# A ConvFFN whose down projection takes seven products of quarter matrices instead of eight, for 16 of 22 feature blocks

## The chip, the cores and the metric

The kernel runs on one core of one Trainium2 chip, as one launch. The metric is the device time of that launch in microseconds (us). Each engine of the core works through its own queue of instructions in order: TensorE (PE) does the matrix products and loads their weights (PEld), VectorE (DVE), ScalarE (ACT) and GpSimd (POOL) do elementwise work, and SyncE (SP) and POOL issue DMAs.

## The reference, cut to what matters

Two layers with different mixers; each is followed by the same ConvFFN. A prompt of 512 tokens and 8 samples of 8 tokens go through the same weights, 576 tokens in all.

```python
D_MODEL = 1024
D_FF = ((8 * D_MODEL // 3 + 255) // 256) * 256      # 2816 = 22 blocks of 128

def conv_ffn(h, hist, w_gate, w_up, conv_w, conv_b, w_down):
    gate = h @ w_gate
    padded = jnp.concatenate([hist, gate], axis=1)
    gc = causal_dwconv(padded, conv_w, conv_b)
    y = (jax.nn.silu(gc) * (h @ w_up)) @ w_down
    return y, padded[:, -(FFN_CONV_WIDTH - 1):]
```

## The kernel before, in words

Everything is kept with features on the 128 partitions and the 576 tokens along the free axis, in two halves of 288 (`HB`). The running sum lives in eight tiles `self.x[m]` of 128x576. Products are fp32 made of three matmuls on values split in two: a high part (`hi`, a copy that ScalarE rounds) and a low part (`lo`, the rest, subtracted on VectorE): hi·hi, hi·lo and lo·hi, added up in one PSUM bank. Every operand therefore costs one ScalarE and one VectorE instruction before TensorE can use it.

`ffn` handles one layer's ConvFFN. The first blocks of gate and up are done plainly (`lead`). The others go in pairs of feature blocks as **jobs** (class `Strassen`): 19 a layer, a Gate job and an Up job by turns. A job multiplies the two weight blocks with the 1024x576 input in seven products of quarters instead of eight. Its weight sums S1 to S4 are made by DMA: SP loads one quarter from HBM into a slot of SBUF, and POOL issues a second DMA that adds another on top. `alpha`, `beta` and `gamma` split the upper weights, (S1, S2) and (S3, S4) into hi and lo; p1 to p7 are the products, each of 12 matmuls. A Gate job ends in `gate_done` (convolution, SiLU, the new state), an Up job in `up_done`.

The **down projection** of the 22 blocks goes in six parts (`PARTS`): blocks 0 and 1, then four parts of four blocks (2 to 17), and the last four in `out_proj`. `down(p)` is a generator: each step does one output block m and one half of the tokens, and adds the bank to `self.x[m]` on VectorE (`add_x`). The loop over the jobs calls one step after p1, p3, p7 and p5 (`some(1)`), four a job, so a part of 16 steps lies beside four jobs; what is left of the part of blocks 14 to 17 behind the last job is done in one go (`some(16)`).

Weights come through three buffers `wr` (`weights_load`). Smaller things take slots from a list (`S`), 48 and 14 extra, given out in the order in which they were freed; a slot's new writer waits for its last reader. The tile framework orders the instructions of each engine itself, from the order of the code and its own idea of when inputs are there; the first matmul of a product is pinned to the order of the code.

Of the kernel before, what the change touches and what calls it, by code (L numbers as in the profile page):

```python
# [14 lines left out]
P = 128  # L15
# [9 lines left out]
PARTS = ((0, 2), (2, 6), (6, 10), (10, 14), (14, 18), (18, 22))  # L25

# [25 lines left out]
class Strassen:  # L52

    def __init__(self, b, job, n):
        self.b, self.nc, self.job = b, b.nc, job
        s = b.sr
        self.r, self.e, self.a = s[0][:, HALF[0]], s[1][:, HALF[0]], s[1][:, HALF[1]]

    def load(self):
        b = self.b
        up, low = self.job.src
        self.up = b.weights_load(up, 1024)
        s1, s2, s3, s4 = self.s = [b.S(f"st{i}", 512) for i in range(4)]
        for s, first, more in ((s1, low[:, 512:1024], low[:, 0:512]), (s2, up[:, 0:512], s1), (s4, up[:, 512:1024], s2),
                               (s3, up[:, 0:512], low[:, 0:512])):
            self.nc.sync.dma_start(s, first)
            self.nc.gpsimd.dma_start(s, more, accum_op=ADD)  # L69
        self.low = b.weights_load(low[:, 512:1024], 512)  # L70
        self.alpha()

    def sums(self, between=None):
        b = self.b
        if between:
            between()
        self.d = b.S("dh", 512, F32R), b.S("dl", 512, F32R)
        self.split(self.low[:, 0:512], *self.d)
# [22 lines left out]
    def gamma(self):  # L101
        self.w3 = self.two(self.s[3], self.s[2])
        self.b.free(self.s[3], self.s[2])
# [54 lines left out]
class Builder:  # L158
    NSLOT = 48
    EXTRA = 14  # L160

    def __init__(self, nc, tc, d, stack):
# [7 lines left out]
        self.rings = {"mm": [0, 1, 2, 3], "aux": [4, 5, 6, 7]}  # L170
        self.idle = list(range(self.NSLOT))
# [4 lines left out]
    def S(self, name, n=T, dt=F32, rows=P):  # L176

        i = self.idle.pop(0)
# [90 lines left out]
    def weights_load(self, src, n):  # L269
        raw = self.wp.tile([P, 1024], F32, tag="wr", bufs=3, name="wr")  # L270
# [275 lines left out]
    def ffn(self, l, next_norm):  # L546
        nc, d = self.nc, self.d
        self.rings = {"mm": [0, 1, 2, 3, 4, 5], "aux": [6, 7]}
        hist, so = self.S("fhist", NF * 16), self.S("fso", NF * 16)
# [30 lines left out]

        def up_done(f):
            y_of[f] = self.pair("y")
# [143 lines left out]

        todo = [Gate(LEAD_G), Up(LEAD_U)]
# [3 lines left out]
        self.sr = [self.S("st"), self.S("st")]  # L731
        tiles = iter(())
# [7 lines left out]
        for n, job in enumerate(todo + [None]):  # L740
# [35 lines left out]
            if ready < len(PARTS) - 1 and PARTS[ready][1] - 1 in y_of and n < len(todo):  # L776
                some(16)
                tiles = down(ready)
                ready += 1
            prev = new  # L780
        some(16)
        nc.sync.dma_start(d["ffn_s"][l], so)
        nc.sync.dma_start(d["ffn_p"][l], po)
        self.free(so, hist, self.sr, list(self.hq.values()))
# [1139 lines left out]
```

## Time and profile before

| | us |
|---|---|
| median of 3 runs (lowest to highest) | 1482.55 (1481.72 to 1483.52) |
| the profiled execution's own time | 1483.3 |
| its span in the trace | 1481.5 |
| busy in the span: DVE, ACT, POOL | 1119.0, 822.0, 304.1 |
| parts of four blocks beside four jobs, layer 0 | 323.85 to 393.91, to 463.95, to 534.20 |
| the last such part and its rest, layer 0 | 534.20 to 585.20 |
| the same four in layer 1, each from | 1191.47, 1261.54, 1331.41, 1401.49 |

In a row of groups stand the line of the kernel, the engine, the operation, the tile written and those read, the shapes and the count; then busy us and the mean ns of one; then the idle time of the engine before them and what ended it. A row of windows gives the stretch, its length, and the busy us (and instructions) of PE, PEld, DVE, ACT and POOL, then the granted TensorE clock, the DMA share and GB/s. A row of the timeline gives start, duration, engine, line, operation, tiles and count.

### The profile page before, as it was taken

Reading aid. Unit: us, or ns where it says so; the run is one execution under the profiler, and the core shown is the slowest. Engines: PE = TensorE matmul, PEld = TensorE weight load, DVE = VectorE, ACT = ScalarE, POOL = GpSimd, SP = SyncE. Lnnn points to the kernel's source line nnn. Section 1 sums busy time; section 2 is a strip of 40 time slices with the busy share of each in tenths; the row PEclk is TensorE's granted clock in tenths of the full one; section 3 lists DMA queues with packets and bytes.
Section 4 is the critical chain, followed back from the end, with each engine's and each line's share of the span. In section 5 each row is a group of like instructions: output and inputs, shape, how many; then the busy total and the mean of one; then the engine's idle time right before and its main releaser. Section 6 shows DMA issues by size and latency. Waiting matters only on the chain.

```text
span 1481.5 us, 29273 instructions
## 1 busy us (share of the span) xinstructions
PE 1459.2 (99%) x11179; PEld 1389.9 (94%) x11179; DVE 1119.0 (76%) x2121; ACT 822.0 (55%) x1659; POOL 304.1 (21%) x517
## 2 busy tenths in 40 slices
PE   8999999999999999999999999999999999999999
PEld 7967799999999999998988998997999999999998
DVE  7968799876666665878897777776989766666673
ACT  6357467655445543487764665665457554444450
POOL 0026211222222220011203102102022222232300
PEclk9999999999999999999999999999999999999999
DMA  7604553787777772136245245245366787877841
GB/s 228 164 29 118 160 133 100 195 212 197 184 200 197 191 191 69 58 121 199 72 154 178 86 124 165 86 146 166 105 172 176 193 217 184 211 195 179 212 113 65
DMA packets 120779, 227.60 MB, mean 154 GB/s; under 512 B 25518, under 2 KB 32558, under 8 KB 120638
## 3 DMA queue, kind: packets, MB, share of 16 engines
q1 hardware_dynamic: 98750, 185.87, 39.7%
q0 software_dynamic: 21888, 39.86, 16.3%
q8 instruction: 88, 1.44, 0.4%
q14 instruction: 53, 0.43, 0.1%
HBM read 190.54 MB, written 15.21 MB: 139 GB/s over the span
## 4 chain that ended last, share of the span: by engine, by line
PE 86%; DVE 6%; ACT 4%; DMA 2%; issue 1%; SPq 0%; ACTq 0%; POOL 0%; DVEq 0%
PE mm L313 15%; PE mm L317 15%; PE mm L316 15%; PE x L113 5%; PE x L116 5%; PE x L117 5%; PE y L116 3%; PE y L117 3%; PE y L113 3%; PE mm L622 2%; PE mm L618 2%; PE mm L621 2%; PE z L116 1%; PE z L113 1%; PE z L117 1%; DMA acb<-acd 1%
## 5 line engine op out<-in xcount | busy, mean ns | idle before, releaser
L313 PE MATMUL mm<-hh,wh 128*128 128x288 f32 x864 | 261.0, 303 | 6.0 <-ACT wh L284 5.4
L316 PE MATMUL mm<-hl,wh 128*128 128x288 f32 x864 | 258.8, 300 | 0.9 <-DVE hl L801 0.8
L317 PE MATMUL mm<-hh,wl 128*128 128x288 f32 x864 | 257.5, 298 | 0.5 <-DVE wl L285 0.5
L497 DVE TENSOR_TENSOR x<-x,mm 128x288 f32<-128x288 f32 x288 | 128.6, 449 | 77.6 <-PE mm L317 76.3
L313 PEld LDWEIGHTS mm<-hh,wh 128*128 128x128 f32 x864 | 163.6, 190 | 14.3 <-ACT wh L284 5.9
L313 PE MATMUL mm<-yh,vh 128*128 128x288 f32 x576 | 170.0, 295 | 0.0
L316 PE MATMUL mm<-yl,vh 128*128 128x288 f32 x576 | 169.9, 295 | 0.0
L317 PE MATMUL mm<-yh,vl 128*128 128x288 f32 x576 | 169.8, 295 | 0.0
L316 PEld LDWEIGHTS mm<-hl,wh 128*128 128x128 f32 x864 | 163.5, 189 | 4.4 <-issue 1.6
L317 PEld LDWEIGHTS mm<-hh,wl 128*128 128x128 f32 x864 | 163.6, 189 | 3.5 <-issue 1.6
L284 ACT ACTIVATE wh<-wr 128x1024 fp32r<-128x1024 f32 (+1 forms) x97 | 101.6, 1048 | 102.6 <-PE mm L316 79.0
L285 DVE TENSOR_TENSOR wl<-wr,wh 128x1024 fp32r<-128x1024 f32 (+1 forms) x97 | 119.5, 1236 | 36.3 <-ACT wh L284 35.5
L82 ACT ACTIVATE wh<-st 128x512 fp32r<-128x512 f32 x152 | 91.3, 626 | 57.8 <-PE z L116 36.0
L69 POOL DMA_DIRECT2D st<-st x76 | 67.5, 889 | 262.8 <-DMA st<-st 65.5
L313 PE MATMUL mm<-yh,wh 128*128 128x288 f32 x384 | 115.9, 302 | 0.7 <-DVE x L497 0.7
L317 PE MATMUL mm<-yh,wl 128*128 128x288 f32 x384 | 115.0, 300 | 0.0
L316 PE MATMUL mm<-yl,wh 128*128 128x288 f32 x384 | 114.9, 300 | 0.0
L83 DVE TENSOR_TENSOR wl<-st,wh 128x512 fp32r<-128x512 f32 x152 | 101.3, 688 | 15.9 <-ACT wh L82 12.3
L316 PEld LDWEIGHTS mm<-yl,vh 128*128 128x128 f32 x576 | 108.4, 188 | 0.0
L317 PEld LDWEIGHTS mm<-yh,vl 128*128 128x128 f32 x576 | 108.3, 188 | 0.0
L313 PEld LDWEIGHTS mm<-yh,vh 128*128 128x128 f32 x576 | 108.3, 188 | 0.0
L573 DVE SCALAR_TENSOR_TENSOR gconv<-gbuf,par,gconv 128x592 f32<-128x592 f32 x88 | 73.0, 832 | 32.2 <-ACT gconv L571 31.6
(409 smaller groups left out, 4306.4 us busy)
## 6 DMA issues: line engine op xcount, KB each, us to landing
st<-in_w_up SPq DMA_DIRECT2D x80, 256.0 KB, 4.3
wr<-in_w_down SPq DMA_DIRECT2D x80, 256.0 KB, 3.5
wr<-in_w_in_o SPq DMA_DIRECT2D x40, 512.0 KB, 3.6
st<-st POOLq DMA_DIRECT2D x76, 256.0 KB, 4.7
st<-in_w_gate SPq DMA_DIRECT2D x72, 256.0 KB, 4.6
wr<-in_w_gate SPq DMA_DIRECT2D x26, 512.0 KB, 4.3
wr<-in_w_up SPq DMA_DIRECT2D x24, 512.0 KB, 4.1
st<-in_w_up POOLq DMA_DIRECT2D x40, 256.0 KB, 4.7
```

The source lines that it names most:

```text
L82: nc.scalar.activation(hi, src, AF.Copy)
L83: nc.vector.tensor_tensor(lo, src, hi.bitcast(F32), op=SUB)
L113: m = nc.tensor.matmul(out, hi[:, ws], xh, start=first and k == 0, stop=False, skip_group_check=skip)
L116: nc.tensor.matmul(out, hi[:, ws], xl, start=False, stop=False, skip_group_check=skip)
L117: nc.tensor.matmul(out, lo[:, ws], xh, start=False, stop=k == 3, skip_group_check=skip)
L284: nc.scalar.activation(hi[:, a:b], raw[:, a:b], AF.Copy)
L285: nc.vector.tensor_tensor(lo[:, a:b], raw[:, a:b], hi[:, a:b].bitcast(F32), op=SUB)
L313: first = nc.tensor.matmul(out, hi[:, ws], xh[:, sl], start=i == 0, stop=False)
L316: nc.tensor.matmul(out, hi[:, ws], xl[:, sl], start=False, stop=False)
L317: nc.tensor.matmul(out, lo[:, ws], xh[:, sl], start=False, stop=i == n - 1)
L497: nc.vector.tensor_tensor(self.x[m][:, sl], self.x[m][:, sl], p[:, :HB], op=ADD)
L573: nc.vector.scalar_tensor_tensor(cv[:, :592], g[:, k:592 + k], w(k), cv[:, :592], op0=MUL, op1=ADD)
```

## The change

For the four parts of four blocks (`SEVEN`), `down7` replaces `down`. It takes two output blocks m and m+1 and four feature blocks at a time as a 2x2 matrix of quarters, and the activations as 2x2 too (two blocks by two, left and right half of the tokens), and makes the result in seven products of 6 matmuls where there were eight. For this it adds weight sums S1 to S4 on VectorE, sums of activations (T1 to T4, once a part), splits of each, and more additions to `self.x`: a product that belongs to two quarters of the result is continued in its bank after it has been added once. A pair of output blocks takes four yields: two products, two, two, one. `up_done` splits only the left half of a part's first two blocks; the rest is split in `down7` (`operand`).

To make room, the jobs keep S3 and S4 in the buffer of the upper weights (`ring_up`, two of the three `wr`): POOL's DMA adds onto them after `alpha` has read them. The jobs' last quarter (`low`) takes a slot, the new state `so` lies in the tile of the old one (`hist`), tiles wider than 576 take odd slots only, and there are 15 extra slots.

```diff
 PARTS = ((0, 2), (2, 6), (6, 10), (10, 14), (14, 18), (18, 22))
+SEVEN = (1, 2, 3, 4)
...
     def load(self):
...
-        self.up = b.weights_load(up, 1024)
-        s1, s2, s3, s4 = self.s = [b.S(f"st{i}", 512) for i in range(4)]
-        for s, first, more in ((s1, low[:, 512:1024], low[:, 0:512]), (s2, up[:, 0:512], s1), (s4, up[:, 512:1024], s2),
-                               (s3, up[:, 0:512], low[:, 0:512])):
-            self.nc.sync.dma_start(s, first)
+        self.up = b.weights_load(up, 1024, b.ring_up)
+        s1, s2 = [b.S(f"st{i}", 512) for i in range(2)]
+        s3, s4 = self.up[:, 0:512], self.up[:, 512:1024]
+        self.s = s1, s2, s3, s4
+        self.nc.sync.dma_start(s1, low[:, 512:1024])
+        self.nc.sync.dma_start(s2, up[:, 0:512])
+        self.low = b.S("a22", 512)
+        self.nc.sync.dma_start(self.low, low[:, 512:1024])
+        self.alpha()
+        for s, more in ((s1, low[:, 0:512]), (s2, s1), (s3, low[:, 0:512]), (s4, s2)):
             self.nc.gpsimd.dma_start(s, more, accum_op=ADD)
-        self.low = b.weights_load(low[:, 512:1024], 512)
-        self.alpha()
...
-    EXTRA = 14
+    EXTRA = 15
...
-        i = self.idle.pop(0)
+        i = next((i for i in self.idle if n <= T or i % 2), self.idle[0])
+        self.idle.remove(i)
...
-        hist, so = self.S("fhist", NF * 16), self.S("fso", NF * 16)
+        hist = so = self.S("fhist", NF * 16)
...
+        def operand(name, src, sign=1.0):
+            q = self.S(name, T, F32R)
+            hi, lo = q[:, 0:HB], q[:, HB:T]
+            nc.scalar.activation(hi, src, AF.Copy, scale=sign)
+            if sign < 0:
+                nc.vector.scalar_tensor_tensor(lo, src, sign, hi.bitcast(F32), op0=MUL, op1=SUB)
+            else:
+                nc.vector.tensor_tensor(lo, src, hi.bitcast(F32), op=SUB)
+            return q
+
         def up_done(f):
+            for p in SEVEN:
+                a, b = PARTS[p]
+                if a <= f < b:
+                    y_of[f] = operand("yq", sl_of[f][:, HALF[0]]) if f < (a + b) // 2 else None
+                    return
...
+            def go():
+                for m in range(0, 8, 2):
+                    a11, a12, a21, a22 = [raw[m][:, i * n:i * n + n] for i in range(4)]
+                    w = self.single(raw[m][:, 0:2 * n]) if m else first
+                    s12, s43 = self.S("sd", 512), self.S("sd", 512)
+                    s1, s2, s4, s3 = s12[:, 0:n], s12[:, n:2 * n], s43[:, 0:n], s43[:, n:2 * n]
+                    nc.vector.tensor_tensor(s1, a21, a22, op=ADD)
+                    nc.vector.tensor_tensor(s2, s1, a11, op=ADD)
+                    x, z = self.ps("dx"), self.pm()
+                    product(x[:, :HB], w, 0, t["B11"], True)
+                    add(m, 0, x, ADD)
+                    product(z[:, :HB], w, n, t["B21"], True)
+                    add(m, 0, z, ADD)
+                    w = self.single(s12[:, 0:2 * n])
+                    nc.vector.tensor_tensor(s3, a11, a21, op=ADD)
+                    nc.vector.tensor_tensor(s4, a12, s2, op=ADD)
+                    self.free(s12)
+                    last = self.S("dd", 512, F32R)
+                    dh, dl = last[:, 0:n], last[:, n:2 * n]
+                    nc.scalar.activation(dh, a22, AF.Copy)
+                    nc.vector.tensor_tensor(dl, a22, dh.bitcast(F32), op=SUB)
+                    load(m + 2)
+                    if m == 0:
+                        for name in ("T1", "B22", "T2"):
+                            quarters_of(name)
+                    yield
+                    y = self.ps("dy")
+                    product(y[:, :HB], w, 0, t["T1"], True)
+                    add(m + 1, 1, y, SUB)
+                    product(x[:, :HB], w, n, t["T2"], False)
+                    add(m, 1, x, ADD)
+                    w = self.single(s43[:, 0:2 * n])
+                    self.free(s43)
+                    if m == 0:
+                        quarters_of("T3")
+                    yield
+                    product(y[:, :HB], w, 0, t["B22"], False)
+                    add(m, 1, y, ADD)
+                    product(x[:, :HB], w, n, t["T3"], False)
+                    add(m + 1, 1, x, SUB)
+                    if m == 0:
+                        quarters_of("T4")
+                    yield
+                    product(x[:, :HB], (dh, dl), 0, t["T4"], False)
+                    add(m + 1, 0, x, SUB)
...
+                    yield
+            return go()
...
+        self.ring_up, self.ring_wr = self.ring_wr[:2], self.ring_wr[2:]
...
-                tiles = down(ready)
+                tiles = (down7 if ready in SEVEN else down)(ready)
```

`quarters_of` makes the sums and operands: T1 two sums and two operands, B22 two operands, T2 four sums and two operands, T3 two operands, T4 two sums and two operands. `product` is six matmuls: two feature blocks by the three hi and lo combinations.

How instructions stand now is shown at two places. The first is VectorE where the part of blocks 6 to 9 begins, from the last addition of the part ahead (`x_84` is `self.x[7]`) to the first addition of the new one (`x_77` is `self.x[0]`); L89 and L83 are splits of a job's weights, L303 and L294 splits of down weights. Before:

```order
L497 TENSOR_TENSOR x_84<-x_84,mm 128x288
L294 TENSOR_TENSOR vl<-wr,vh 128x512
L672 SCALAR_TENSOR_TENSOR gsilu<-x,gsilu 128x288
L336 TENSOR_TENSOR yl<-gsilu,yh 128x576
L83 TENSOR_TENSOR wl<-st_4932,wh 128x512
L83 TENSOR_TENSOR wl<-st_4933,wh 128x512
L497 TENSOR_TENSOR x_77<-x_77,mm 128x288
```

The same place in the changed kernel (L800 is the addition, L819, L820 and L825 make S3, S4 and the low part of the last quarter, L597 splits an operand, L777 is a sum of activations):

```order
L800 TENSOR_TENSOR x_84<-x_84,dx 128x288
L303 TENSOR_TENSOR vl<-sd,vh 128x512
L820 TENSOR_TENSOR sd<-wr,sd 128x256
L696 SCALAR_TENSOR_TENSOR gsilu<-x,gsilu 128x288
L825 TENSOR_TENSOR dd<-wr,dd 128x256
L597 TENSOR_TENSOR yT<-gsilu,yT 128x288
L597 TENSOR_TENSOR yq<-gsilu,yq 128x288 x3
L777 TENSOR_TENSOR gsilu<-gsilu 128x288 x2
L89 TENSOR_TENSOR dl<-a_4965,dh 128x512
L777 TENSOR_TENSOR gsilu<-gsilu 128x288 x2
L800 TENSOR_TENSOR x_77<-x_77,dx 128x288
```

Between the two additions stood five instructions and stand thirteen; the two splits of S1 and S2 of the job (`wl<-st`) have moved behind the addition, and the rest of the new sums and splits of the part stands ahead of this place and behind it.

The second place is POOL's queue over one Up job beside a part of four blocks; `st` are the job's slots, and `wr` in the changed kernel is the buffer of its upper weights. Before:

```order
L69 DMA st_4503<-in_w_up 128x512
L69 DMA st_4501<-in_w_up 128x512
L69 DMA st_4502<-st_4501 128x512
L69 DMA st_4504<-st_4502 128x512
L69 DMA st_4722<-in_w_gate 128x512
```

The changed kernel:

```order
L76 DMA st_4518<-in_w_up 128x512
L568 MEMSET gbuf 128x2
L569 COPY gbuf<-fhist 128x8x2
L76 DMA st_4519<-st_4518 128x512
L76 DMA wr<-in_w_up 128x512
L76 DMA wr<-st_4519 128x512
```

S3's addition (`<-in_w_up`) stood first and now stands third, behind S1 and S2; on SP the loads of S3 and S4 are gone, two of 256 KB a job, 76 in all.

More of the change, by code (lines that the diff above doesn't have):

```diff
@@ L77, in sums @@
         self.d = b.S("dh", 512, F32R), b.S("dl", 512, F32R)
-        self.split(self.low[:, 0:512], *self.d)
+        self.split(self.low, *self.d)
+        b.free(self.low)
     def split(self, src, hi, lo):
@@ L102, in gamma @@
         self.w3 = self.two(self.s[3], self.s[2])
-        self.b.free(self.s[3], self.s[2])
     def product(self, bank, w, col, q, first):
@@ L170, in __init__ @@
         self.rings = {"mm": [0, 1, 2, 3], "aux": [4, 5, 6, 7]}
+        self.ring_wr = [0, 1, 2]
         self.idle = list(range(self.NSLOT))
@@ L267, in setup, with weights_load @@
         nc.scalar.activation(self.warm, self.eps, AF.Sqrt)
-    def weights_load(self, src, n):
-        raw = self.wp.tile([P, 1024], F32, tag="wr", bufs=3, name="wr")
+    def weights_load(self, src, n, ring=None):
+        ring = ring or self.ring_wr
+        ring.append(ring.pop(0))
+        raw = self.wp.tile([P, 1024], F32, tag=f"wr{ring[-1]}", bufs=1, name="wr")
         srcs = src if isinstance(src, list) else [src]
@@ L725, in down, with product @@
             return go()
+        def product(out, w, col, xs, first):
+            hi, lo = w
+            for k, q in enumerate(xs):
+                ws = slice(col + k * P, col + k * P + P)
+                m = nc.tensor.matmul(out, hi[:, ws], q[:, 0:HB], start=first and k == 0, stop=False, skip_group_check=not first)
+                if k == 0:
+                    self.tc.keep_in_program_order(m)
+                nc.tensor.matmul(out, hi[:, ws], q[:, HB:T], start=False, stop=False, skip_group_check=not first)
+                nc.tensor.matmul(out, lo[:, ws], q[:, 0:HB], start=False, stop=k == len(xs) - 1, skip_group_check=not first)
@@ L781, in ffn @@
         some(16)
+        self.ring_wr = self.ring_up + self.ring_wr
         nc.sync.dma_start(d["ffn_s"][l], so)
         nc.sync.dma_start(d["ffn_p"][l], po)
-        self.free(so, hist, self.sr, list(self.hq.values()))
+        self.free(hist, self.sr, list(self.hq.values()))
         if next_norm:
```

41 lines of the change are left out of this document (added).

## The prediction

> **What bounds the kernel now.** I read the page's busy shares first, then the windows of the parts that the change touches, then single instructions there.
>
> ```profile
> PE 1459.2 (99%) x11179; PEld 1389.9 (94%) x11179; DVE 1119.0 (76%) x2121; ACT 822.0 (55%) x1659; POOL 304.1 (21%) x517
> L313 PE MATMUL mm<-yh,vh 128*128 128x288 f32 x576 | 170.0, 295 | 0.0
> L497 DVE TENSOR_TENSOR x<-x,mm 128x288 f32<-128x288 f32 x288 | 128.6, 449 | 77.6 <-PE mm L317 76.3
> ```
>
> TensorE is busy nearly all the time, the matmuls of the down projection wait for nothing (0.0), and the additions behind them wait for TensorE (76.3 us): VectorE stands ready and TensorE is late. The 295 ns are no price, since matmuls overlap. The price is the distance of two starts. The next rows are the windows of one whole part (blocks 6 to 9), of its second job, and of two earlier stretches; then, from the timeline, TensorE's first down matmul of that job.
>
> ```profile
> 393.91:463.95 70.04, 70.04 (x531) 70.04 (x529) 46.77 (x85) 34.77 (x62) 20.18 (x35) 1.00 0.78 194
> 411.43:428.95 17.52, 17.52 (x135) 17.52 (x133) 11.98 (x23) 8.39 (x15) 3.85 (x5) 1.00 0.73 194
> 230.00:260.00 30.00, 30.00 (x228) 30.00 (x227) 29.65 (x64) 24.25 (x53) 6.35 (x10) 1.00 0.34 100
> 1110.00:1130.00 20.00, 20.00 (x153) 20.00 (x152) 20.00 (x39) 17.74 (x37) 5.82 (x9) 1.00 0.53 142
> ```
> ```profile
> 411.43 0.29 PE L313 MATMUL mm<-yh,vh 128*128 128x288 f32 x1
> ```
>
> A job with its four steps is 84 + 48 = 132 matmuls by the code (the window counts those cut by its edges too) and takes 17.52 us, so **one matmul costs 17.52/132 = 0.1327 us**. The granted clock is 1.00. VectorE works 46.77 of 70.04 us. The two other windows show that TensorE can run at its full rate (228 in 30 us) while VectorE has no gap at all, at least for 20 to 30 us.
>
> **The change part by part.** *TensorE.* A part of four blocks had 16 steps of 12 matmuls, 192; now 4 pairs of output blocks by 7 products of 6, 168. That is 24 less in each of four parts in two layers, 192 matmuls, and 192 x 0.1327 = **25.5 us** if TensorE goes on at its rate. A part takes 70.04 - 24 x 0.1327 = 66.9 us then, a job 16.7.
>
> *VectorE* pays for it. The prices, from the groups of the window 393.91 to 463.95 and from a run of instructions with no gap:
>
> ```profile
> L83 DVE TENSOR_TENSOR wl<-st,wh 128x512 fp32r<-128x512 f32 x17 | 11.4, 689 | 0.9 <-ACT wh L82 0.2
> L497 DVE TENSOR_TENSOR x<-x,mm 128x288 f32<-128x288 f32 x16 | 7.2, 449 | 5.2 <-PE mm L317 5.2
> L573 DVE SCALAR_TENSOR_TENSOR gconv<-gbuf,par,gconv 128x592 f32<-128x592 f32 x8 | 6.7, 833 | 3.9 <-ACT gconv L571 3.8
> L83 DVE TENSOR_TENSOR wl<-wr,wh 128x1024 fp32r<-128x1024 f32 x4 | 4.9, 1218 | 0.0
> L336 DVE TENSOR_TENSOR yl<-gsilu,yh 128x576 fp32r<-128x576 f32 x4 | 3.0, 754 | 1.6 <-ACT yh L335 1.6
> L83 DVE TENSOR_TENSOR dl<-wr,dh 128x512 fp32r<-128x512 f32 x4 | 2.8, 690 | 7.7 <-ACT dh L82 4.7 <-DMA st<-st 3.0
> L635 DVE TENSOR_TENSOR gbuf<-st,y 128x224 f32<-128x224 f32 x2 | 0.8, 382 | 0.0
> ```
> ```profile
> 406.05 0.44 DVE L659 TENSOR_TENSOR st<-st,z 128x288 f32<-128x288 f32 x1
> 406.41 0.68 DVE L83 TENSOR_TENSOR wl<-st,wh 128x512 fp32r<-128x512 f32 x1
> 407.01 0.45 DVE L661 TENSOR_TENSOR gsilu<-gsilu,st 128x288 f32<-128x288 f32 x1
> 407.38 0.68 DVE L83 TENSOR_TENSOR wl<-st,wh 128x512 fp32r<-128x512 f32 x1
> 407.99 0.44 DVE L497 TENSOR_TENSOR x<-x,mm 128x288 f32<-128x288 f32 x1
> ```
>
> Starts follow each other 0.08 us closer than the durations say: 288 wide costs 0.37 in a full queue, 512 wide 0.60, 576 wide 0.67. No instruction of 256 is in these rows; it lies between 224 (382 ns) and 288 (449), I take 0.41 and so 0.33.
> - Gone per part: 16 additions x 0.37, 8 splits of 512 x 0.60, 4 splits of 576 x 0.67 = 13.4 us.
> - New per part: 28 additions x 0.37, 12 splits of 512 x 0.60, 16 weight sums and 4 splits of 256 x 0.33, 14 operand splits and 8 sums of 288 x 0.37 = 32.4 us.
>
> That is **19.0 us more VectorE work a part**. What a part needed before without gaps, by its counts and the same prices: 28 splits of 512 (sixteen `wl`, four `dl`, eight of the down weights; 16.8), 32 instructions of 288 (11.8), 8 of 592 (6.0), 4 of 1024 (4.6), 4 of 576 (2.7), 8 small ones (1.7): 43.6. So 62.6 of 66.9 us now, 94%. It fits, with 4 us to spare in a part and none to waste. It isn't even: counted in the changed order between the splits of the upper weights, the four jobs of a part need 19.3, 13.6, 15.0 and 14.7 us against 16.7 of TensorE. The job in which a part begins is 2.6 over.
>
> What takes that up is the lead that VectorE has over TensorE, in the timeline of the job from 411.43: the split of the next job's upper weights and those of S1 and S2, and the first matmuls that need them.
>
> ```profile
> 411.39 1.28 DVE L83 TENSOR_TENSOR wl<-st,wh 128x512 fp32r<-128x512 f32 x2
> 419.38 1.22 DVE L83 TENSOR_TENSOR wl<-wr,wh 128x1024 fp32r<-128x1024 f32 x1
> 420.98 0.30 PE L113 MATMUL y<-hqT,wh 128*128 128x288 f32 x1
> 427.35 0.29 PE L113 MATMUL x<-hqB,wh 128*128 128x288 f32 x1
> ```
>
> The one is done at 420.6 and used at 427.35 (6.7 us early), the other at 412.7 and used at 420.98 (8.3). An overrun of 2.6 goes into it, and the next job, 3.1 under, pays it back. The new waits are tighter: where a bank is added and then continued, TensorE has only one job's product and one of its own in between (18 x 0.1327 = 2.4 us) until it needs VectorE's 0.45. In the worst place of the order, from a part's last addition to the first of the next, stand 13 instructions of 5.2 us, and TensorE has three products of a job and one of the part, 42 matmuls or 5.6 us. It just fits.
>
> The stall left over is what I can't read. Bounds: nothing, or the whole overrun at the six part beginnings with a 19.3 us job (6 x 2.6 = 15.6), and at each layer's last part, whose rest has no jobs beside it, up to 2 us each. The leads are more than twice the overrun, so I take a value near the lower end, **3 us**.
>
> *ScalarE* gets 4 splits of 512, 4 of 256 and 14 of 288 for 4 of 576: by its rows some 7 us a part on 34.77. It stays under 42 of 66.9, behind TensorE. The scheduler also puts three more table loads into the second mixer, by this row 1.28 each on ScalarE; 0 to 4 us, I take **0.5**.
>
> ```profile
> L1295 ACT ACT_TABLE_LOAD x9 | 11.5, 1283 | 0.2
> ```
>
> *DMA, POOL, buffers.* Two loads of 256 KB a job go; nothing waited for them on TensorE, so 0. S3's addition waits for `alpha` now, and S1 of the next job stands behind it in POOL's queue. `alpha` is done 6.7 us ahead of its use, and S3 is needed a whole job later (p3), so I take 0; the other end is the second rival. The state in one tile, odd slots and the 15th slot: 0, POOL's copies are in the same number.
>
> **Sum.** The profiled execution took 1483.3 us. 1483.3 - 25.5 + 3 + 0.5 = 1461.3. The median of the runs is 0.75 below that execution, so **1461 us**.
>
> **The rivals.** *VectorE becomes the bound.* If each instruction kept VectorE for its whole duration, the 46.77 busy of a part and the additions by durations (38.9 for 15.7, 23.2 more) would be 70.0 us, and a part would take as long as before: 1483. The same comes out if the wait ahead of `dl` (7.7 us a part, for ScalarE and DMA) stays beside 62.6: 70.3. The starts 0.36 to 0.37 us apart behind durations of 0.44 speak against the first, the lead against the second. In between lies a share of it, 1468 to 1479.
>
> The Trainium skill, VectorE: DVE Perf Modes, section The DRAIN you can't avoid, says that a next instruction doesn't start until the pipe is empty. By that rule in its strict form the change would give nothing, 1483. This trace disagrees, by the starts just named.
>
> *S1 and S2 come too late, and the kernel is slower.* The changed program has fewer slots idle (down to 1 from 4 by the allocation in the code), and in two of four jobs of a part S1's slot comes free only when the former job's S1 has been split. The chain from there is a load, two additions and the splits:
>
> ```profile
> st<-in_w_up SPq DMA_DIRECT2D x80, 256.0 KB, 4.3
> st<-st POOLq DMA_DIRECT2D x76, 256.0 KB, 4.7
> st<-in_w_up POOLq DMA_DIRECT2D x40, 256.0 KB, 4.7
> ```
>
> 4.3 + 4.7 + 4.7 + 1.3 = 15.0 us, under a job's 16.7. But if POOL stands 6.7 us at S3's addition, waiting for `alpha`, it is 21.7, 5.0 over in each of two jobs; the lead of 8.3 takes most, and 1.7 a part would be lost, 8 parts x 1.7 = 14. It decides where the lead isn't there: 10 a part, 80 us, less 25.5, is 1538; at half of that VectorE's queue, which waits in order, stands 40 us and the time is 1498. For it: POOL's waits for DMA. Against: 15.0 is under 16.7, and the lead.
>
> *The products aren't fewer:* the built order has 192 matmuls less, so no chance.
>
> **How the numbers follow.** Forecast (1456 to 1468) 0.61; VectorE in part the bound (1468 to 1479) 0.12; VectorE the bound (1479 to 1487) 0.11, of it 0.03 for whole durations and 0.08 for the wait ahead of `dl`; S1 and S2 late (1487 to 1540) 0.14; more than the full saving 0.02. A measurement of this kernel can tell 0.2%, 3 us, from no change. Faster: 0.61 + 0.12 + 0.02 = 0.75; the same: 0.09; slower: 0.14 + 0.02 = 0.16. The range runs from the full 25.5 and a little, 1455, to 1483, where VectorE is just the bound; some 0.8 lies in it.
>
> **What would show it.** In the windows of the parts: a job beside a part at 16.7 to 16.9 us, 28 additions a part, VectorE 62 to 66 us busy of 67, and no idle time of note ahead of the new products on TensorE. Wrong is the sum of VectorE if TensorE waits for additions (`x`) or operands; wrong is the lead if jobs at a part's beginning take over 17.5 us; the second rival shows as VectorE waiting for `st<-st`. The forecast fails if the jobs keep 17.5 us.

## The result and the profile after

The changed kernel took 1543.36 us (median of 4 runs, 1536.71 to 1548.75) against 1482.13 for the kernel before on the same chip: a ratio of 1.0413 (95% interval 1.0366 to 1.0460). **It is 4.1% slower; 1461 was forecast.** The profiled execution's span is 1538.8 us, 57.3 more than before.

The busy shares of the page, then the windows: the whole part of blocks 6 to 9, one job in which TensorE stopped, and the job behind it.

```profile
PE 1462.0 (95%) x10987; PEld 1377.7 (90%) x10987; DVE 1257.9 (82%) x2553; ACT 869.1 (56%) x1806; POOL 305.4 (20%) x517
```
```profile
379.48:451.49 72.01, 68.18 (x507) 67.07 (x505) 64.03 (x139) 40.91 (x81) 18.66 (x33) 1.00 0.68 161
470.04:491.96 21.92, 18.94 (x128) 18.33 (x127) 18.30 (x43) 12.29 (x26) 4.40 (x10) 0.92 0.51 136
491.96:508.60 16.64, 16.61 (x126) 16.37 (x125) 16.04 (x34) 9.36 (x20) 4.65 (x8) 1.00 0.74 166
```

The 192 matmuls are gone, and a job that nothing disturbs takes 16.64 us where it took 17.52. But the part takes 72.01 (before 70.04), and a job can take 21.92. TensorE, 99% busy before, is 95% busy.

Where the time went is seen job by job. For 36 jobs (18 a layer) I took the length from the first matmul of one job's p2 to that of the next, the number of matmuls times 0.1327, the gaps (distances of two starts over 0.3 us, less 0.133), and what is left:

| 36 jobs, us | length | at full rate | gaps | rest: slower starts |
|---|---|---|---|---|
| before | 598.75 | 598.74 | 0 | 0.0 |
| after | 654.95 | 578.04 | 59.7 | 17.2 |

So 20.7 of the 25.5 us saved lie in these jobs, **59.7 us of gaps and 17.2 of slow matmuls are new**, and 56.2 of the 57.3 are accounted for. Of these 76.9 us lost, 20.2 lie in the first jobs of the two layers, before the first of the new products (at 333.1 and 1229.1 us); there TensorE waits within the jobs' own products and at the plain down products of blocks 0 and 1. The waits of TensorE (us in all, times, longest), and the group that waits longest on ScalarE, in the changed kernel and, as `dh<-wr`, before:

```profile
PE dx L755 <- DVE x L800: 12.8, 8, 2.3
PE dy L755 <- ACT vh L302: 11.0, 6, 5.8
PE y L118 <- ACT st L125: 7.6, 2, 4.4
```
```profile
L88 ACT ACTIVATE dh<-a 128x512 fp32r<-128x512 f32 x38 | 24.0, 631 | 101.0 <-DMA a<-in_w_up 72.2 <-DMA a<-in_w_gate 20.8 <-DVE yT L597 2.4
```
```profile
L82 ACT ACTIVATE dh<-wr 128x512 fp32r<-128x512 f32 x38 | 24.0, 630 | 51.5 <-DMA wr<-in_w_gate 27.3 <-DMA wr<-in_w_up 22.6 <-DVE wl L83 1.5
```

TensorE waits for several things, ScalarE mostly for one: the job's last quarter, `a`. How the one becomes the other is in the timeline of the job from 470.04 (rows of other instructions left out):

```profile
476.35 0.33 SPq L282 DMA_DIRECT2D wr<-in_w_gate  x1
476.77 0.40 SPq L73 DMA_DIRECT2D a<-in_w_up  x1
...
482.88 0.29 PE L759 MATMUL dy<-yT,vl 128*128 128x288 f32 x1
482.92 0.63 ACT L88 ACTIVATE dh<-a 128x512 fp32r<-128x512 f32 x1 [2.81 <-DMA a<-in_w_up]
483.45 0.76 ACT L593 ACTIVATE yT<-gsilu 128x288 fp32r<-128x288 f32 x2
483.58 0.69 DVE L89 TENSOR_TENSOR dl<-a,dh 128x512 fp32r<-128x512 f32 x1 [2.23 <-ACT dh L88]
...
484.93 0.44 DVE L800 TENSOR_TENSOR x<-x,dx 128x288 f32<-128x288 f32 x1
...
485.52 0.37 PE L755 MATMUL dx<-yT,vh 128*128 128x288 f32 x1 [2.34 <-DVE x L800]
486.53 0.61 PE L758 MATMUL dx<-yT,vh 128*128 128x288 f32 x1 [0.64 <-DVE yT L595]
```

The load of `a` is issued at 476.77, and ScalarE's wait for it ends at 482.9. ScalarE stands at `dh` 2.81 us, VectorE at `dl` behind it 2.23, and in both queues stand, in order, what TensorE needs next: the split of `yT` and the addition to `x` after which a bank may be continued. That addition comes at 484.93, and TensorE has stopped after 482.88.

### The profile page after: what moved, and what is told of

The parts are those of the page before. It is cut to its first block, busy times and chain, and to the rows that moved or that the text cites. A ratio compares the mean times of both kernels' runs of the same rounds, so it can differ in the third digit from the quotient of the medians.

```text
span 1538.8 us, 29389 instructions
## 1 busy us (share of the span) xinstructions
PE 1462.0 (95%) x10987; PEld 1377.7 (90%) x10987; DVE 1257.9 (82%) x2553; ACT 869.1 (56%) x1806; POOL 305.4 (20%) x517
## 3 DMA queue, kind: packets, MB, share of 16 engines
q0 software_dynamic: 21888, 39.86, 15.6%
## 4 chain that ended last, share of the span: by engine, by line
PE 56%; DVE 18%; DMA 15%; ACT 5%; issue 5%; SPq 1%; POOL 0%; ACTq 0%; DVEq 0%; POOLq 0%
PE mm L322 9%; PE mm L326 9%; PE mm L325 9%; DMA a<-in_w_up 5%; PE x L118 2%; PE x L121 2%; PE x L122 2%; DMA st<-st 2%; DMA st<-in_w_up 2%; DVE wl L89 2%; DVE gconv L582 1%; PE dx L758 1%; DVE x L800 1%; PE dx L755 1%; PE dx L759 1%
## 5 line engine op out<-in xcount | busy, mean ns | idle before, releaser
L294 DVE TENSOR_TENSOR wl<-wr,wh 128x1024 fp32r<-128x1024 f32 (+1 forms) x97 | 121.8, 1259 | 31.3 <-ACT wh L293 30.9
L89 DVE TENSOR_TENSOR wl<-wr,wh 128x512 fp32r<-128x512 f32 (+1 forms) x114 | 95.9, 860 | 1.3 <-ACT wh L88 0.6
L88 ACT ACTIVATE wh<-wr 128x512 fp32r<-128x512 f32 (+1 forms) x114 | 83.2, 763 | 21.9 <-PE z L121 13.1
L118 PE MATMUL x<-hqT,wh 128*128 128x288 f32 x304 | 92.4, 304 | 0.0
L121 PE MATMUL x<-hqT,wh 128*128 128x288 f32 x304 | 92.4, 304 | 0.0
L122 PE MATMUL x<-hqT,wl 128*128 128x288 f32 x304 | 92.0, 302 | 0.0
L506 DVE TENSOR_TENSOR x<-x,mm 128x288 f32<-128x288 f32 x160 | 70.3, 447 | 25.7 <-PE mm L326 25.4
L88 ACT ACTIVATE dh<-a 128x512 fp32r<-128x512 f32 x38 | 24.0, 631 | 101.0 <-DMA a<-in_w_up 72.2
L322 PEld LDWEIGHTS mm<-yh,wh 128*128 128x128 f32 x384 | 72.2, 188 | 4.1 <-issue 1.7
L1722 POOL TENSOR_TENSOR h<-h,cds 128x512 f32<-128x512 f32 x32 | 42.7, 1363 | 164.1 <-PE pyo L1716 164.1
L326 PEld LDWEIGHTS mm<-yh,wl 128*128 128x128 f32 x384 | 72.2, 188 | 1.0 <-issue 0.4
```

What stands on the lines that cost most here:

```text
L88: nc.scalar.activation(hi, src, AF.Copy)
L89: nc.vector.tensor_tensor(lo, src, hi.bitcast(F32), op=SUB)
L118: m = nc.tensor.matmul(out, hi[:, ws], xh, start=first and k == 0, stop=False, skip_group_check=skip)
L121: nc.tensor.matmul(out, hi[:, ws], xl, start=False, stop=False, skip_group_check=skip)
L122: nc.tensor.matmul(out, lo[:, ws], xh, start=False, stop=k == 3, skip_group_check=skip)
L294: nc.vector.tensor_tensor(lo[:, a:b], raw[:, a:b], hi[:, a:b].bitcast(F32), op=SUB)
```

## The experiments

A part below is the one of blocks 6 to 9 in layer 0; gaps and slow starts are sums over the 36 jobs as above. Each run's ratio is to the kernel before on the same chip.

One caution goes for all of them. The framework orders the instructions of each program anew, and an edit that changes a slot, a width or a load's place can move others with it. By the sequences of tiles in the traces, of the runs that edit the changed kernel's loads, slots or sums only e5 has PE, ACT, DVE and SP issue in the changed kernel's order. In e15, for instance, some 330 of 2553 VectorE instructions and 200 of 559 issues on SyncE stand elsewhere; e11's order isn't that of the kernel before either. So apart from e5, a difference of two runs is that of an edit together with a new order.

| run | us | ratio (95%) | gaps + slow |
|---|---|---|---|
| e1 room edits alone | 1494.97 | 1.0099 (1.0070 to 1.0128) | 5.2 + 2.3 |
| e4 seven products, loads as before | 1514.56 | 1.0221 (1.0171 to 1.0271) | 40.7 + 14.5 |
| e7 one part of seven products | 1480.89 | 0.9995 (0.9986 to 1.0004) | 0.7 + 0.4 |
| e3 no sums of activations | 1548.34 | 1.0459 (1.0415 to 1.0504) | 64.3 + 22.2 |
| e6 narrow additions | 1555.10 | 1.0502 (1.0481 to 1.0523) | 67.9 + 20.2 |
| e5 no accumulating DMAs | 1468.85 | 0.9919 (0.9897 to 0.9941) | 6.2 + 1.0 |
| e2 last quarter split later | 1550.68 | 1.0475 (1.0431 to 1.0520) | 67.1 + 20.0 |
| e8 last quarter loaded first | 1501.07 | 1.0133 (1.0112 to 1.0155) | 29.6 + 6.3 |
| e10 room edits alone, last quarter first | 1484.64 | 1.0026 (1.0015 to 1.0036) | 2.1 + 0.0 |
| e11 before with three slots less | 1531.61 | 1.0340 (1.0297 to 1.0383) | 30.9 + 10.0 |
| e12 four slots fewer taken | 1531.52 | 1.0340 (1.0323 to 1.0356) | 47.7 + 15.1 |
| e13 the same, last quarter first | 1525.01 | 1.0290 (1.0272 to 1.0309) | 41.3 + 18.1 |
| e15 three slots for the loads | 1505.39 | 1.0166 (1.0146 to 1.0186) | 31.9 + 9.3 |
| e16 the same, last quarter first | 1541.58 | 1.0405 (1.0350 to 1.0461) | 61.8 + 17.5 |
| e17 four slots for the loads | 1504.92 | 1.0149 (1.0132 to 1.0166) | 35.0 + 8.6 |
| e18 the same, last quarter first | 1529.28 | 1.0307 (1.0264 to 1.0351) | 51.0 + 20.3 |
| e9 sums on GpSimd | 1595.61 | 1.0775 (1.0758 to 1.0791) | 99.5 + 35.5 |
| e14 last quarter loaded once | 1590.05 | 1.0738 (1.0708 to 1.0767) | 92.0 + 29.7 |

### The two halves of the change, one at a time

The first run keeps the room edits and takes the old down projection.

```diff
-SEVEN = (1, 2, 3, 4)
+SEVEN = ()
```

> Room edits alone: S3 and S4 in the upper weights' buffer, the last quarter in a slot, one ring of two and one of one, 15 extra slots, but the down projection as before (no part in seven products). Theory Q (the loss is made by loads that stand in SP's and POOL's queues behind others, so that ScalarE waits in order for the last quarter): slower than before, 1500 to 1530, with ScalarE idle ahead of dh for a<-in_w over 60 us. Theory V (VectorE is overloaded where a part begins): as before, 1480 to 1485.

```profile
ACT dh L88 <- DMA a<-in_w_gate: 59.6, 13, 6.9
ACT dh L88 <- DMA a<-in_w_up: 24.3, 15, 4.3
```

ScalarE's waits for the last quarter are there already, 83.9 us against 93.0 in the changed kernel. The kernel is 15 us slower with them (under the 1500 that theory Q named; 7.5 us of it lie in the 36 jobs, ahead of the parts of four blocks); with the seven products too, which should save 25.5, it is 61 slower. So the room edits make the transfer late. That the seven products make its lateness dear fits the timeline above, but not the 20.2 us ahead of the first new product, and e5 below shows a late `a` that costs little.

The second run has the seven products with the loads of before (four slots for S1 to S4, three common `wr`, 15 extra slots, the state in one tile); only the last quarter's split goes into the next job, ahead of p3, since the slots don't reach otherwise.

```diff
-                new.sums(between)
+                between()
...
             if prev:
+                prev.sums()
```

> Seven products in the four parts as in the changed kernel, but the jobs' loads as before (S1 to S4 in four slots, the last quarter in one of the three shared buffers), with the last quarter split late as in e2 to free two slots. Theory Q: faster than before, 1458 to 1475. Theory V: 1520 to 1545.

It is 2.2% slower, between the two forecasts, with ScalarE waiting for other transfers (below). The room edits aren't the whole cause either.

```profile
ACT wh L84 <- DMA st<-st: 28.7, 14, 4.4
ACT dh L84 <- DMA wr<-in_w_up: 20.4, 6, 5.9
ACT vh L299 <- DMA wr<-in_w_down: 15.7, 5, 4.8
```

In the same form with one part only, blocks 14 to 17, and the split of the last quarter where it was:

```diff
-SEVEN = (1, 2, 3, 4)
+SEVEN = (4,)
```

> The kernel before with its own loads and slots (four slots for S1 to S4, low quarters in the three shared weight buffers), and the seven products in one part only, f 14 to 17 of each layer. 48 matmuls less a layer pair, 2 x 24 x 0.1327 = 6.4 us. If the loss of the changed kernel comes from the transfers and the tight buffers (Q, I): about 1474 to 1478 us, no PE gap over 1 us in that part. If seven products cost by themselves what the four parts with the old loads cost (34 us over 8 parts, 4.2 us each, two parts here): about 1488.

No gain (1474 to 1478 was expected), though the jobs lose 1.1 us in all. Only 1.6 of the 6.4 us saved lie beside jobs; the others come behind the last job, where TensorE now waits for splits (PE in 556 to 640 us, where nothing over 0.5 us stood before):

```profile
PE mm L319 <- ACT hh L341: 1.7, 3, 1.1
PE mm L323 <- DVE wl L291: 1.7, 2, 0.9
PE mm L322 <- DVE hl L342: 1.0, 3, 0.3
```

### Is it VectorE's load?

First the 8 sums of activations a part are left out of the changed kernel (the products then take unsummed values), later all 28 additions to `x` and those 8 sums are made 32 columns wide instead of 288; the expectation says 256, which is wrong.

```diff
-                nc.vector.tensor_tensor(out, x, y, op=op)
```
```diff
-                nc.vector.tensor_tensor(x, x, bank[:, :HB], op=op)
+                x = x[:, 0:32]
+                nc.vector.tensor_tensor(x, x, bank[:, 0:32], op=op)
```

> The changed kernel without the eight sums of activations of a part (T1 to T4 are split from the unsummed tiles, so the result isn't the reference's): 8 x 0.37 = 3.0 us less of VectorE where a part begins, 24 us in all. Theory V: 1543 less 20 to 30 us. Theory Q: under 10 us less.

> The changed kernel with the 28 additions to x and the 8 sums of activations of each of the four parts made over 32 columns instead of 256 (the other columns are left out). Same instructions in the same order, same waits and transfers; VectorE has some 9.6 us less a part (about 53 of 66.9 instead of 62.6). Theory I (it takes a late transfer and a full VectorE): 1480 to 1505 us, ScalarE still waits for a<-in_w_up, PE waits for VectorE less than half as long. Theory Q (the late transfers alone): 1530 us or more. Theory V (VectorE alone): about 1460 to 1480.

Neither gains anything. The part's window with narrow additions:

```profile
379.88:457.25 77.37, 70.91 (x507) 69.65 (x505) 56.32 (x139) 40.55 (x81) 20.03 (x33) 0.96 0.62 150
```

VectorE is busy 56.32 us instead of 64.03, and the part takes 77.37 instead of 72.01. That speaks against VectorE's load as the cause, alone (theory V of these expectations) or as one of two conditions (theory I). It doesn't settle it: the "same order" of the expectation didn't hold, since some 770 VectorE instructions and 110 issues on SyncE stand elsewhere in e6. The next run settles theory V.

### Is it the transfers?

The four accumulating DMAs of each job are left out; S1 to S4 are then plain quarters.

```diff
-        for s, more in ((s1, low[:, 0:512]), (s2, s1), (s3, low[:, 0:512]), (s4, s2)):
-            self.nc.gpsimd.dma_start(s, more, accum_op=ADD)
```

> The changed kernel without the four accumulating DMAs of each up or gate job (S1 to S4 are then plain loaded quarters, so this part of the computation is left out). VectorE, ScalarE and TensorE issue what they issue in the changed kernel; only the long chain of transfers through the two upper-weight buffers and the four slots is gone, so that each buffer comes free as soon as its splits are done. Theory I (a late transfer holds ScalarE's in-order queue, and VectorE at 94% of TensorE's pace cannot make up what is lost; it takes both): 1460 to 1495 us, ScalarE's wait for a<-in_w_up falls from 72 us to under 20. Theory V (VectorE's load in the parts is enough by itself): 1520 us or more, with PE still waiting for x and yT. Theory Q (the transfers alone): about 1460, with no waits of PE.

```profile
362.76:431.01 68.25, 67.68 (x506) 66.97 (x505) 64.44 (x139) 41.15 (x81) 4.48 (x17) 1.00 0.33 109
```

1468.85 us, 12.4 below the kernel before and 74.5 below the changed one. The same 139 VectorE instructions take 64.44 of 68.25 us, 94%, and TensorE is held up by 1.4 us a part against 66.9. So the new work fits beside TensorE: **VectorE's load alone is not the cause**, and what doesn't fit is the four additions by DMA. The orders on PE, ACT, DVE and SP and the slots are those of the changed kernel, so these cost 74.5 us only together with the additions.

A late `a` alone isn't the price either. ScalarE still waits 28.4 us for it here, more than in e8 below (24.4), yet gaps and slow starts are 7.2 us against 35.9; a wait of 3.5 us that ends at 481.0 lies in a job of 16.99 us, where the 2.81 of the timeline above lay in one of 21.92. This run takes away the chain of additions, its hold on the buffers and half the DMA share (0.33; 0.68 in the changed kernel's part) at once; the next ones ask which of these it is.

### Where in the queue a load stands

`a` is loaded behind the next upper weights and two more quarters. Splitting it later, ahead of p3 of the next job (the edit of e4, made in the changed kernel), takes the wait off `dh`:

> The changed kernel, but each job's last quarter is split into dh and dl in the next job, ahead of p3, and no longer ahead of p1. The same work. Theory Q: the wait of ScalarE for a<-in_w falls from 93 us to under 30 and the time to 1480 to 1510. Theory V: 1535 to 1550, the jobs at the beginning of a part still take 19 to 22 us.

```profile
ACT wh L88 <- DMA st<-st: 57.0, 17, 7.2
ACT vh L302 <- DMA wr<-in_w_down: 17.4, 8, 4.5
ACT wh L88 <- DMA st<-in_w_gate: 12.2, 8, 3.5
```

The wait on `a` is gone, and ScalarE waits for S2 instead: no gain, where theory Q expected 1480 to 1510. Loading it earlier is another matter:

```diff
+        self.low = b.S("a22", 512)
+        self.nc.sync.dma_start(self.low, low[:, 512:1024])
         self.up = b.weights_load(up, 1024, b.ring_up)
...
-        self.low = b.S("a22", 512)
-        self.nc.sync.dma_start(self.low, low[:, 512:1024])
```

> The changed kernel with one transfer moved: the last quarter (a<-in_w) is issued ahead of the next job's upper weights on SyncE's queue instead of behind them and the two st quarters. Theory I and Q with SyncE's order as the cause: ScalarE's wait for a<-in_w falls from 93 us to under 30 and the time to 1490 to 1520. If the slot is what comes late (the wait for the slot's last reader, not the order of the queue): the wait moves to the upper weights that now stand behind it, and the time stays at 1535 to 1550.

> The room edits alone (no seven products, as in the run that gave 1495), with the last quarter issued ahead of the upper weights. If SyncE's order is what cost the room edits their 15 us: 1480 to 1484. If it is the slots and the chain of additions through the two upper buffers: 1490 or more. The seven products with this order stand at 1501, 16 us above e5.

```profile
ACT wh L88 <- DMA st<-st: 20.6, 7, 4.3
ACT dh L88 <- DMA a<-in_w_gate: 16.7, 5, 6.6
ACT dh L88 <- DMA a<-in_w_up: 7.7, 8, 1.8
```

With the seven products this one transfer's place is worth 42 us (1543.36 to 1501.07), and with the room edits alone it brings their loss from 15 us down to 3.5. In the first the wait for `a` falls from 93.0 to 24.4 us. So a load's place in SyncE's queue matters, where what stands ahead waits for its buffer (the SPq rows below), though the other engines' orders changed with it.

### Which slot a load gets

Slots go out in the order in which they were freed in the code. The kernel before, with three slots less and nothing else:

```diff
-    EXTRA = 14
+    EXTRA = 11
```

> The kernel before with three slots less (11 instead of 14 of the wide ones), so that only one stays free at the tightest place, as in the changed kernel. All else is the same. If scarce slots by themselves make the transfers late: 1490 us or more, with ScalarE waiting for DMAs over 60 us (before 50). If not: 1480 to 1484.

```profile
SPq L68 <- DVE gconv L573: 161.4, 25, 14.5
```
```profile
SPq L68 <- DVE gconv L573: 33.1, 17, 2.8
```

50 us slower, without any of the change. The rows are SyncE's waits ahead of a load of an `st`, with three slots less and in the kernel before: the load is handed a slot whose last reader is the convolution of a gate row, up to 14.5 us away on VectorE. So are slots what the seven products lack? In the next run T3 and T4 are left out and T1 and T2 used twice, so that four slots a part fewer are taken:

```diff
-                    t[name] = [operand("yT", u[:, right]) for u in us]
+                    t[name] = t["T1"]
...
-                    t[name] = [operand("yT", combine(v[:, left], v[:, right], v[:, left], SUB)) for v in vs]
+                    t[name] = t["T2"]
```

> The changed kernel in which the sixth and seventh operand of a part (T3 and T4) are not formed and those of T1 and T2 stand in their place (this part of the computation is left out): the same products, the same loads, the same order on SyncE and the same accumulating DMAs, but four slots a part fewer are taken. VectorE has 6 instructions a part less, which e3 and e6 showed to be worth nothing. If scarce slots are what makes the transfers late in the parts: 1490 to 1515 us. If it is the order on SyncE and the two upper buffers, whatever the slots: 1530 or more.

> The same four slots fewer in the version with the last quarter issued ahead of the upper weights (1501 with all slots taken; T3 and T4 are again left out). If slots and order are the whole cause, what e5 has without any accumulating DMA: 1465 to 1475. If the chain of four additions costs by itself: 1485 or more.

```profile
SPq L73 <- DVE gconv L582: 109.2, 11, 13.7
```

Only 12 us better, and with the last quarter first 24 us worse than with all slots taken. Again a load waits for `gconv`: more free slots only change which slot is next. So the next runs ask about that. Three (then four) slots are set aside for the loads of S1, S2 and `a`:

```diff
-        i = next((i for i in self.idle if n <= T or i % 2), self.idle[0])
-        self.idle.remove(i)
+        if self.own and name in ("st0", "st1", "a22"):
+            i = self.own.pop(0)
+        else:
...
-                self.idle.append(self.used.pop(id(t))[0])
+                i = self.used.pop(id(t))[0]
+                (self.own if i in self.load_slots else self.idle).append(i)
```

> The changed kernel with three slots set aside for the loads of S1, S2 and the last quarter, so that such a load waits for nothing but the same load's readers one job earlier; the other tiles have three slots less to take from (at the tightest place none stays free). The same instructions in the same order on every engine. If it is which slot a load is handed (one whose last reader stands late on VectorE, such as gconv, x or a bank's copy), not how many are free: 1480 to 1510, and SyncE's waits at the st and a loads fall under 20 us in 260:560. If the number of free slots, or the chain through the two upper buffers, decides: 1530 or more.

```profile
375.07:443.21 68.14, 67.59 (x506) 66.89 (x505) 63.72 (x137) 40.74 (x81) 15.47 (x27) 1.00 0.68 165
```

38 us gained (1543.36 to 1505.39) with every instruction and every transfer still there. The part takes 68.14 us, as without the accumulating DMAs, at the changed kernel's DMA share of 0.68: **in this part it isn't the amount of traffic or of work, it is when they come**. That it is the slot's last reader is not shown. The sign that was named for it missed: SyncE's waits at the loads of S1, S2 and `a` in 260 to 560 us are 134 us, not under 20; in the changed kernel they were 120.5. The order isn't the same either (above). ScalarE's wait for `a` falls from 93.0 to 51.2. All jobs of layer 0 from 341 us on run at 16.65 to 18.1. Of the 41.3 us of gaps and slow starts left, 25 lie in six jobs around the layers' first parts and 7 in two others.

> The same three slots set aside, in the version with the last quarter issued ahead of the upper weights (1501 without). If late slots and the order on SyncE's queue are the whole loss: 1468 to 1480, as without the accumulating DMAs. If the chain of four additions, some 5 us each, costs by itself: 1490 or more.

```profile
SPq L73 <- DMA wr<-st: 96.3, 29, 5.6
SPq L72 <- DVE wl L89: 87.0, 23, 11.2
SPq L72 <- DMA st<-st: 58.4, 19, 5.8
```

The two remedies don't add up: 1541.58. With this order each of the three loads gets the slot of its own forerunner, and S2's load (L73) waits for the addition of S4 that still reads it. Four slots keep that apart:

> The changed kernel with four slots set aside for the loads of S1, S2 and the last quarter (e15 had three; where no other is free, another tile may take one of them). With three, handed round in turn, the last quarter of a job gets the slot of the job before's S2, which the addition of S4 reads last; with four it gets that of S1. Everything else as in the changed kernel. If late slots are the loss: the two jobs per layer that still lose 4 to 6 us ahead of the first part come back and the time falls to 1470 to 1485. If the chain of four additions by itself is too long for jobs of 14.3 us: 1500 or more.  e15 stands at 1505.

> Four slots set aside for the loads and the last quarter issued ahead of the upper weights. Alone, the slots gave 1505 and the order 1501; three slots with this order gave 1542, since each load then had the slot of its own forerunner, which the addition of S4 still reads. If the two causes are separate and add up: 1465 to 1480, faster than the kernel before. If both only treat the same late transfers: 1490 to 1505. If the order needs the general slots: 1520 or more.

Neither is a gain: 1504.92, as with three, and 1529.28. The first came out as its expectation said for a chain of four additions that is too long for jobs of 14.3 us, the second as for an order that needs the general slots. In e17 the jobs around the first part get shorter, but two others take 25.4 and 24.5 us; in e18 ScalarE waits for `a` 42.3 us again.

### Other ways to the sums

GpSimd can add in place of the DMAs (S3 and S4 onto the upper weights, S2 as S3 + a22):

```diff
-            self.nc.gpsimd.dma_start(s, more, accum_op=ADD)
+            self.nc.gpsimd.tensor_tensor(out, x, y, op=ADD)
```

> The changed kernel with the last quarter and the other lower quarter loaded ahead of the upper weights, and the four sums made by GpSimd instructions instead of accumulating DMAs: S3 and S4 in the place of the upper weights as now, S2 as S3 + a22. Three loads a job instead of four and four additions; each sum costs GpSimd some 1.25 us by h<-h 128x512 (39.2 us for 32), 5 us of a job's 16.7. Theory Q (the chain of transfers behind S1 to S4 is what costs, at some 5 us each, one after the other): 1465 to 1475 us, as without the sums (1468.85). Against it: GpSimd's instructions stand behind its copies that wait for gate rows, or lengthen VectorE's: 1480 to 1500.

```profile
383.51:466.05 82.54, 72.95 (x506) 70.22 (x505) 78.99 (x139) 41.15 (x81) 27.49 (x34) 0.96 0.23 77
```
```profile
L88 DVE TENSOR_TENSOR dl<-a,dh 128x512 fp32r<-128x512 f32 x38 | 38.6, 1016 | 6.1 <-ACT dh L87 6.1
```
```profile
L89 DVE TENSOR_TENSOR dl<-a,dh 128x512 fp32r<-128x512 f32 x38 | 26.0, 684 | 34.4 <-ACT dh L88 32.2 <-DMA st<-in_w_up 2.0
```
```profile
L88 DVE TENSOR_TENSOR wl<-wr,wh 128x512 fp32r<-128x512 f32 x76 | 121.2, 1623 | 1.2
```
```profile
L89 DVE TENSOR_TENSOR wl<-wr,wh 128x512 fp32r<-128x512 f32 x76 | 49.6, 682 | 0.5
```

The slowest of all. The same 139 VectorE instructions now take 78.99 us of the part's 82.54: the split `dl` takes 1016 ns (first row) where it took 684 in the changed kernel (second), and the split of S3 and S4 1623 (third row) for 682 (fourth). Here VectorE is 96% busy in the part, because instructions beside GpSimd's additions take longer (last section).

Last, `a` is not loaded: its split is made from S1's slot ahead of the addition.

```diff
-        self.low = b.S("a22", 512)
-        self.nc.sync.dma_start(self.low, low[:, 512:1024])
         self.alpha()
+        self.d = b.S("dh", 512, F32R), b.S("dl", 512, F32R)
+        self.split(s1, *self.d)
```

> The changed kernel with a22 loaded once: its split is made from the slot of S1 before a21 is added to it, so one load and one slot a job go, nothing is left out, and SyncE's queue holds no transfer behind the upper weights but S2's. S1's addition waits for the split in return (some 2 us: ACT dh and DVE dl 128x512). If order and slots decide: 1470 to 1500. If a later start of the chain S1, S2, S4 decides: 1530 or more.

```profile
ACT wh L84 <- DMA st<-st: 43.5, 25, 5.6
ACT wh L84 <- DMA st<-in_w_gate: 43.5, 12, 6.2
ACT wh L84 <- DMA st<-in_w_up: 40.5, 10, 4.9
```

One load and one slot less, and 47 us slower than the changed kernel: the chain S1, S2, S4 starts later, and ScalarE waits for its results at S1 and S2.

## Why the prediction was wrong

- **TensorE: right in count and in the job.** 192 matmuls are gone, and an undisturbed job takes 16.64 us (16.7 was said). But 36 of them lie behind the last jobs, and e7 shows no gain there.
- **VectorE: right in size.** 62.6 us a part by starts was said; the window has 64.03 by durations, and e5 and e15 show parts of 68.25 and 68.14 us with that work in them. Rival 1 (VectorE the bound) is refuted for this change by e5, which has all of that work in the same order. The lead takes up most of the overrun of 2.6 us when nothing else is late, not all: in e5 the jobs at a part's beginning take 17.7 to 17.8 us, over the 17.5 that was named as a sign against it.
- **ScalarE: right.** 40.91 us a part (under 42 was said).
- **The stall of 3 us: a size.** In e5, where no sum is waited for, gaps and slow starts beside jobs are 7.2 us. With what is lost outside the jobs, 12.4 of the 25.5 us are gained, so 13.1 are lost where 3 was taken, still inside the bounds that were named (15.6, and up to 2 at each layer's last part).
- **"DMA, POOL, buffers": the step that failed.** "Two loads of 256 KB a job go; nothing waited for them on TensorE, so 0", and 0 for S3's addition behind `alpha` and for the new slots. With the same order on four engines and the same slots, the changed kernel takes 74.5 us less without the additions by DMA (e5). That nothing waited was true of TensorE and the wrong question. ScalarE already waited 51.5 us at `dh`, 50 of it for the load; the row is above, and the prediction's own `dl<-wr` row showed 7.7 us a part of the same. Nobody paid for it: the down products read operands that were ready long before. The change put onto that queue, behind `dh`, splits and additions that TensorE needs within a few matmuls, and tightened slots and buffers so that the loads came later. e1 shows the lateness alone (84 us of waiting, 15 us of time), the timeline one case of its price beside the new products.
- **The second rival had the side and the root, not the wait.** It named fewer idle slots and the chain of two additions, at a chance of 0.14 and up to 1540. But it was priced as S1 and S2 late against VectorE's lead of 8.3 us. What ScalarE waited for most in the changed kernel was the last quarter (93.0 us; 9.6 for `st<-st`); "VectorE waiting for `st<-st`" did not show. Its reasons against (15.0 us under 16.7) took each slot to be free when the code frees it; e11 shows waits up to 14.5 us for a slot's reader.
- **Slow matmuls, 17.2 us, were in no sum.**

**What stays open.** e5 shows that the additions by DMA, in the room they were given, cost it. In e8 and e15 the same additions stand at 32 and 37 us over e5 instead of 74.5. But how the 61 us divide between SyncE's order, the slots, the two upper buffers and the order of instructions that comes with each edit can't be said: the remedies don't add up (e16, e18). A rival stands beside them. By their expectations e13, e16 and e17 came out as if the chain of four additions were too long by itself. In e15's part it isn't (68.14 us), but 25 of the 41.3 us left in e15 lie around the layers' first parts, where jobs are shorter (14.3 to 16.7 us undisturbed); no run shortens the chain alone. A free order of transfers that reaches e5's 1468.85 with the sums made was not found: no version that computes everything is faster than the kernel before.

## What to carry to other kernels

Before putting work on an engine that is "not the bound", read what its in-order queue already waits for: a wait that costs nothing can be paid as soon as something urgent stands behind it, and its sum doesn't tell the price (28.4 us in e5 cost little). When slots are handed out in the code's order, a tile saved or added changes which late reader every later load waits for; look at what each load waits for, not only at the number of free slots. Slots of their own for three loads went with 38 us less here, and with 41 more under another order of loads. Where a framework orders the instructions, compare the orders of two runs before a difference is put down to the edit. Price a stop of TensorE at more than its length, if the granted clock falls behind it.

## What the hardware showed

**A short stop also costs clock.** Windows of 4 us around the stop of the timeline above (the clock is the third number from the end), then three matmuls behind it:

```profile
481.00:485.00 4.00, 2.18 (x17) 1.94 (x15) 1.77 (x5) 2.08 (x6) 0.32 (x2) 1.00 0.60 222
485.00:489.00 4.00, 2.84 (x11) 2.66 (x12) 4.00 (x13) 2.25 (x6) 0.38 (x2) 0.68 0.30 97
489.00:493.00 4.00, 4.00 (x29) 4.00 (x28) 3.55 (x9) 2.52 (x5) 1.20 (x3) 0.89 0.43 117
```
```profile
488.62 0.44 PE L118 MATMUL x<-hqT,wh 128*128 128x288 f32 x1
488.86 0.44 PE L121 MATMUL x<-hqT,wh 128*128 128x288 f32 x1
489.10 0.44 PE L122 MATMUL x<-hqT,wl 128*128 128x288 f32 x1
```

After two stops of 2.34 and 0.64 us, matmuls start 0.24 us apart instead of 0.13, for some 3 us, until 489.8. Less was enough elsewhere in the same run: the first window below holds stops of 1.27 and 0.19 us, and the next has half the clock throughout.

```profile
1367.08:1370.49 3.41, 1.95 (x13) 1.47 (x12) 3.41 (x9) 1.84 (x4) 1.11 (x3) 1.00 0.53 94
1370.49:1373.90 3.41, 3.41 (x16) 3.41 (x16) 1.77 (x5) 0.21 (x1) 0.00 (x0) 0.50 0.98 271
```

The Trainium skill, TensorE: Matmul & The Clock Gate, section Wait — 56ns, not 53.3ns?, gives the distance of cold matmuls as the columns over 1.2 GHz, by estimate 0.240 us for 288; the trace agrees (0.24). The Trainium skill, on the same page, section HAM oscillation — how this bites in real kernels, names idle gaps over about 3.4 us as what to avoid; here shorter stops, 1.27 and 0.19 us, were enough.

**GpSimd's additions hold up VectorE instructions with two inputs from SBUF.** `dl` went from 684 to 1016 ns (above), with the same shape and operands. The mean mixes two kinds: the 26 of 38 that meet no addition of GpSimd take 679 ns on average, the 12 that lie beside one for over half of their time 1745. The additions `x<-x,dx`, with one input in PSUM, take 444 ns in e9 and 447 in the changed kernel. The Trainium skill, SBUF — State Buffer, section Who interferes with whom, says that a VectorE instruction with two inputs in SBUF contends with a GpSimd instruction that reads SBUF; e9 agrees.
